# Rows scaled in place and turned by plain transposes at the start of an encoder layer

## The chip, the core and the metric

The kernel runs on one core of one Trainium2 chip. The core has five engines, each with its own queue, worked through in order: TensorE (PE, matmuls; the loading of its weights is listed apart, as PEld), VectorE (DVE), ScalarE (ACT), GpSimd (POOL) and SyncE (SP, which here only issues transfers). PE, DVE and ACT share the banks of PSUM; tiles lie in SBUF; large data lie in DRAM and come and go by DMA. The metric is the time of one execution on the device, in microseconds (us); lower is better.

## The reference

One layer of an encoder for a sequence of 1024 rows and 2048 columns, in 32-bit floats:

```
mod = silu(c) @ w_ada + b_ada;  shift, scale, gate = split(mod, 3)
h = rmsnorm(x, pre_g) * (1 + scale) + shift
proj = h @ w_in                      # q, k, v, gate_a, u, gate_p: 4608 columns
y_a = windowed_gqa(q, k, v, bias, sink) * silu(gate_a)
y_p = multiscale_pool(u) * silu(gate_p)
g = sigmoid(h @ w_merge + b_merge)   # 4096 columns
x + gate * rmsnorm((g_a * (y_a @ w_br_attn) + g_p * (y_p @ w_br_pool)) @ w_out, post_g)
```

For this case only the first two lines and the beginning of the third matter: each row of x is divided by the root of the mean of its squares, turned so that the columns lie on the partitions, and then scaled and shifted per column by numbers that are themselves sums over a 2048-row matrix.

## The kernel before, in words

**Numbers and products.** A 32-bit float is split into a high part (fp32r) and a low part, `split` (L96 on ACT, L97 on DVE), and a product is three matmuls: high by high, high by low, low by high. The large products use Strassen's scheme with seven products for a 2 by 2 block product. For that the turned rows h are kept as seven operands, `MOVING` (B11, T3, T2, B21, T4, T1, B22), each with four steps `j` of two column tiles; the weights are summed and split as they come (`strassen`, matmuls in L248). Nothing of this can start for a step `j` before its columns of x have been normed, turned and modulated (`fill`, L587, for j = 1, 2, 3; `fill_half` and `fill_sums`, L606 and L620, for j = 0).

**The start.** SP issues in this order (L655 on): the first 512 rows of x in sixteen tiles of 256 KB; sixteen tiles of w_ada for modulation group 0; four transfers of early weights (`wide`); claims of tiles; the other 512 rows of x; w_ada for group 1; raw weights for the ramp pairs 4 and 5; w_ada for group 2; raw weights 6; w_ada for group 3; raw weights 7.

A row block `si` has 128 rows and four tiles. `norm_rows` (L414) squares two of them on ACT (L419) and two on DVE (L421), adds up (L423), takes the root on ACT (L426) and the reciprocal on DVE (L427), and multiplies the identity by it (`turn`, L431). The first 512 rows are then turned by real matmuls against that scaled identity (`turn_rows`, L433, matmuls L439), which scales and transposes at once; only the first 1024 columns are turned here. A 32-bit matmul of this kind appears as two records. Of the other 512 rows, column tiles 0 and 1 are turned in the same way (`turn_first`, L449), row block by row block, and tiles 2 to 7 are scaled in place on ACT (`scale_rows`, L457) and turned later by plain transposes (`turn_later`, L463, one record each).

The sums over w_ada for a group run on PE (`modulation`, L506, matmuls named GEMV at L516), four steps of four tiles, then a copy, four transposes (PM) and three small steps on DVE; they give the columns `modc` with which h is scaled and shifted.

While data still arrive, four pairs of weight columns are multiplied with step j = 0 alone by plain blocks: `plain_block(i, nt, s)` (L691) is six matmuls (L697) into one bank, a copy to an `ev` tile on ACT (L702) or DVE (L700) in turns, and a store by SP (L703). There are eight blocks for the left half (s = 0, the first 512 rows) and eight for the right half (s = 1). Before the change the order is written out from L706 to L760: in the left half two blocks, then one row block's norm, turn and scaling, and so on; in the right half the blocks stand between transposes, the sums of step 0 (`fill_sums`) and the four steps of modulation group 1.

Then `fill(1)` makes the operands of j = 1, and the ramp runs Strassen pairs 4 to 7 with j = 0 and 1 (L768), with steps of modulation groups 2 and 3 called at numbered places (`late_sums`, L673, through `side`); then all eight pairs with the remaining steps j (L777), whose raw weights are asked for at L771; after that everything runs from full operands.

**What sets the order.** Each engine works through its queue in order. An instruction wrapped in `keep` stays in program order among those kept; all others are placed by the framework, where it expects their inputs and their tile to be ready. The norms, turns, plain blocks and their copies are kept, as are the raw weights of the ramp; stores, `fill(1)`, the weight sums and splits of the ramp pairs and the small POOL memsets with which tiles are claimed (L585) are not. Tiles are shared: the pool `big` has 56 slots of 256 KB, in which x, w_ada and the operands follow one another, so a load waits until the earlier user of its slot is done. The pool `ev` has nine tiles for results on their way out. Of PSUM, the tags `mm` and `sc` have two banks each and the two tags in `SEEDED` one each.

```
        for q in (2, 3, 0, 1):
            xt, junk = xts[si, q], xts[si, q | 2]
...
                    keep(nc.tensor.matmul(banks[j][:, m * P:(m + 1) * P], xts[4 * s + m, q][:, j * P:(j + 1) * P],
                                          turn[4 * s + m], start=True, stop=True))
...
        ps = bank(("mm", "sc")[blocks[0] % 2], "PB")
```

Of the kernel before, what the change touches and what calls it, by code (L numbers as in the profile page):

```python
# [13 lines left out]
F32 = mybir.dt.float32  # L14
F32R = mybir.dt.float32r
AF = mybir.ActivationFunctionType
ALU = mybir.AluOpType
# [4 lines left out]
P = 128  # L22
# [16 lines left out]
SEEDED = ("z0", "z1")  # L39
# [4 lines left out]
def encoder_layer(ctx: ExitStack, tc: tile.TileContext, x, c, table, w_ada, b_ada, pre_g,  # L44
# [15 lines left out]
    nc = tc.nc  # L60
# [30 lines left out]
    def keep(ins):  # L91

        tc.keep_in_program_order(ins)
# [314 lines left out]
    def fetch_rows_of_x(s):  # L408
        for si in range(4 * s, 4 * s + 4):
            for q in range(4):  # L410
                xts[si, q] = slot("xt", F32)
                load(xts[si, q], x[si * P:(si + 1) * P, q * 512:(q + 1) * 512])

    def norm_rows(si):  # L414
        ssq = ep.tile([P, 8], F32, tag="ssq", name=f"ssq{si}", bufs=4)
        for q in (2, 3, 0, 1):
            xt, junk = xts[si, q], xts[si, q | 2]
            if q % 2 == 0:
                keep(nc.scalar.activation(junk, xt, AF.Square, accum_out=ssq[:, q:q + 1]))  # L419
            else:  # L420
                keep(nc.vector.scalar_tensor_tensor(junk, xt, 1.0, xt, op0=ALU.mult, op1=ALU.mult,  # L421
                                                    accum_out=ssq[:, q:q + 1]))
# [3 lines left out]
        keep(nc.scalar.activation(ssq[:, 5:6], ssq[:, 4:5], AF.Sqrt, bias=eps_t, scale=1.0 / D))  # L426
        keep(nc.vector.reciprocal(rstd[:, si:si + 1], ssq[:, 5:6]))  # L427
# [5 lines left out]
    def turn_rows(s):  # L433

        for q in range(2):
            banks = [bank(t, "XT1") for t in ("mm", "mm", *SEEDED)]
            for m in range(4):
                for j in range(4):
                    keep(nc.tensor.matmul(banks[j][:, m * P:(m + 1) * P], xts[4 * s + m, q][:, j * P:(j + 1) * P],  # L439
                                          turn[4 * s + m], start=True, stop=True))  # L440
            for j in range(4):
                if j % 2 == 0:
                    keep(nc.vector.tensor_copy(xT[q * 4 + j, s], banks[j]))
                else:
                    keep(nc.scalar.activation(xT[q * 4 + j, s], banks[j], AF.Copy))

    late_banks = {}

    def turn_first(m):  # L449

        for k in range(2):
            if m == 0:
                late_banks[k] = bank(SEEDED[k], "XT1")
            keep(nc.tensor.matmul(late_banks[k][:, m * P:(m + 1) * P], xts[4 + m, 0][:, k * P:(k + 1) * P],
                                  turn[4 + m], start=True, stop=True))

    def scale_rows(si):  # L457

        for q, c0 in ((0, 2 * P), (1, 0)):
            part = xts[si, q][:, c0:512]  # L460
            keep(nc.scalar.activation(part, part, AF.Copy, scale=rstd[:, si:si + 1]))

    def turn_later(k, n):  # L463

        pt = bank(SEEDED[n % 2], "XT2")
        for m in range(4):
            keep(nc.tensor.transpose(pt[:, m * P:(m + 1) * P], xts[4 + m, k // 4][:, k % 4 * P:(k % 4 + 1) * P], ident))
        if n % 2:
            keep(nc.vector.tensor_copy(xT[k, 1], pt))
        else:  # L470
            keep(nc.scalar.activation(xT[k, 1], pt, AF.Copy))

    def ada_tile(j, q):
        at = xa.tile([P, 2, 4, P], F32, tag="xa", name=uid("ada"))
# [22 lines left out]
    def ada_slots(j, kcs=range(KT)):  # L497
        tiles = []
        for kc in kcs:
            tiles.append(slot("ada", F32, (P, 4, P)))  # L500
            load(tiles[-1].rearrange("p (g h) n -> p g (h n)", g=2),
                 w_ada[kc * P:(kc + 1) * P, 0:2 * D].rearrange("p (g n) -> p g n", g=2)
                 [:, :, j * 256:(j + 1) * 256])
        return tiles
# [101 lines left out]
    def fill_half(s):  # L606

        names = ("B11", "B21") if s == 0 else ("B12", "B22")
        for k, name in enumerate(names):
            src = xT[k, 0] if s == 0 else late_banks[k]  # L610
# [5 lines left out]
            keep(nc.vector.tensor_scalar(xT[k, s], src, modc[:, 1, k, 0:1], modc[:, 0, k, 0:1],  # L616
                                         op0=ALU.mult, op1=ALU.add))
            keep(sub(lo, xT[k, s], f32(hi)))
# [39 lines left out]
    fetch_wide(1)  # L658
    claim(0)
    fetch_rows_of_x(1)  # L660
# [13 lines left out]
    side = deque((lambda n=n: [step() for step in late_sums.get(n, ())]) for n in range(26))  # L674

    for si in range(4):
        norm_rows(si)
# [10 lines left out]

    blocks = [0]

    def plain_block(i, nt, s):  # L691

        ps = bank(("mm", "sc")[blocks[0] % 2], "PB")
        whi, wlo = (w[:, :, nt * P:(nt + 1) * P] for w in weights0[i])
        mov = (op["B11"][0], op["B21"][0]) if s == 0 else (right["B12"], op["B22"][0])
        for n, (kh, w, m) in enumerate(((0, whi, 0), (0, wlo, 0), (1, whi, 0), (1, wlo, 0), (0, whi, 1), (1, whi, 1))):
            keep(nc.tensor.matmul(ps, w[:, kh], mov[kh][m], start=n == 0, stop=n == 5, skip_group_check=True))  # L697
        t = ev.tile([P, 512], F32, tag="ev", name=uid("c"))
        if blocks[0] % 2:
            keep(nc.vector.tensor_copy(t, ps))  # L700
        else:
            keep(nc.scalar.activation(t, ps, AF.Copy))  # L702
        store(block(ramp_d[i], 0)(f"{nt + 1}{s + 1}"), t)  # L703
# [5 lines left out]
    wide_weights(0)  # L709
    fill_half(0)  # L710
    wide_weights(1)
    norm_rows(4)
    plain_block(0, 0, 0)
    plain_block(0, 1, 0)
    turn_first(0)
    scale_rows(4)
    wide_weights(2)
    plain_block(1, 0, 0)
    norm_rows(5)
    plain_block(1, 1, 0)  # L720
    turn_first(1)
    scale_rows(5)
    wide_weights(3)
    plain_block(2, 0, 0)
    norm_rows(6)
    plain_block(2, 1, 0)
    turn_first(2)
    scale_rows(6)
    plain_block(3, 0, 0)
    norm_rows(7)  # L730
    plain_block(3, 1, 0)
    turn_first(3)
    fill_half(1)
    scale_rows(7)
    early.close()
    late_k = deque(enumerate(range(2, 8)))

    def turn_next(n):
        for _ in range(n):
            m, k = late_k.popleft()  # L740
            turn_later(k, m)

    plain_block(0, 0, 1)
    turn_next(1)
    plain_block(0, 1, 1)
    turn_next(1)
    fill_sums(0)
    plain_block(1, 0, 1)
    turn_next(2)
    plain_block(1, 1, 1)  # L750
    turn_next(2)
    s0, s1, s2, s3, _ = modulation(1, ada[1].__getitem__, True)
    plain_block(2, 0, 1)
    s0()
    plain_block(2, 1, 1)
    s1()
    plain_block(3, 0, 1)
    s2()
    s3()
    plain_block(3, 1, 1)  # L760
# [920 lines left out]
```

## Time and profile before

| what | value |
|---|---|
| median of 3 runs | 2131.82 us (2131.21 to 2134.06) |
| the profiled execution: its time | 2135.61 us |
| its span in the trace | 2133.8 us |
| PE busy | 2079.5 us, 97% of the span |
| DVE busy | 1554.5 us, 73% |
| ACT busy | 1111.6 us, 52% |
| POOL busy | 33.3 us, 2% |
| moved by DMA | 474.49 MB, mean 222 GB/s |

The profile comes from one execution; its times count from the span's start. Rows of the chain read: start, length, engine, tile and line. Rows of the timeline read: start, length, engine, line, operation, output and inputs, count, and in brackets the idle time before and what ended it. Rows of groups read: line, engine, operation, output and inputs, shape, count, then busy microseconds and the mean nanoseconds of one, then idle time before and its releaser. Rows of the windows read: stretch, length, busy microseconds and instruction counts of PE, PEld, DVE, ACT and POOL, the clock granted to PE (1.00 is full speed), the DMA share and GB/s. Rows of transfers read: destination and source, issuing queue, count, size of one, median us from issue to landing. SPq is SP's queue.

### The profile page before, as it was taken

The numbers are of one execution on the slowest core, as the hardware profiler recorded it, in microseconds if no ns is written. First come the engines' busy times: TensorE is split into PE (matmuls) and PEld (weight loads), VectorE is DVE, ScalarE is ACT, GpSimd is POOL, SyncE is SP. The second block draws the span as 40 slices with busy tenths as digits, with TensorE's granted clock in tenths as the row PEclk, the third lists the DMA queues.
The fourth block names the chain that finished last, engine by engine and source line by source line (L and its number), as shares of the span: only waits on it lengthen the run. The fifth ranks groups of instructions, "written<-read, shape, count | busy, mean of one in ns | idle before, by whom it ended". The sixth has DMA issues, their size and how long they took to land.

```text
span 2133.8 us, 28930 instructions
## 1 busy us (share of the span) xinstructions
PE 2079.5 (97%) x9493; PEld 1709.6 (80%) x9493; DVE 1554.5 (73%) x2790; ACT 1111.6 (52%) x2111; POOL 33.3 (2%) x119
## 2 busy tenths in 40 slices
PE   6789999999999999999999999999999999999998
PEld 4558888788888888888888888888888788888886
DVE  4666778787656686577777777867957977879667
ACT  5553444444475454566665533433655645767654
POOL 0000000000000000000000000010000000000000
PEclk8999999999999999999999999999999999999999
DMA  9855877998776456445555477675754556685897
GB/s 321 270 187 196 266 261 243 321 339 294 232 237 224 132 172 208 152 160 179 176 183 161 139 222 230 220 239 182 243 168 159 183 192 198 212 319 199 299 331 246
DMA packets 305196, 474.49 MB, mean 222 GB/s; under 512 B 24324, under 2 KB 144236, under 8 KB 305045
## 3 DMA queue, kind: packets, MB, share of 16 engines
q1 hardware_dynamic: 299968, 459.89, 64.9%
q0 software_dynamic: 3616, 10.53, 1.3%
q10 hardware_dynamic: 1460, 2.22, 0.3%
q8 instruction: 74, 1.21, 0.2%
q14 instruction: 78, 0.63, 0.1%
HBM read 344.60 MB, written 130.05 MB: 222 GB/s over the span
## 4 chain that ended last, share of the span: by engine, by line
PE 92%; DMA 4%; DVE 3%; ACT 1%; issue 0%; SPq 0%; DVEq 0%; POOL 0%; ACTq 0%; POOLq 0%
PE Z L248 30%; PE X L248 20%; PE V L248 20%; PE Z L1388 2%; PE Z L1390 2%; PE Z L1389 2%; PE X L1389 1%; PE X L1390 1%; PE X L1388 1%; PE V L1389 1%; PE V L1388 1%; PE V L1390 1%; PE PT L1098 1%; DMA ada<-in_w_ada_dram 1%; PE PB L697 1%; DMA xt<-in_x_dram 1%
## 5 line engine op out<-in xcount | busy, mean ns | idle before, releaser
L96 ACT ACTIVATE whi<-raw 128x512 fp32r<-128x512 f32 (+2 forms) x528 | 319.3, 606 | 529.7 <-PE Z L248 261.3
L97 DVE TENSOR_TENSOR wlo<-raw,whi 128x512 fp32r<-128x512 f32 (+2 forms) x528 | 344.2, 655 | 172.1 <-PE Z L248 133.2
L97 DVE TENSOR_TENSOR wlo<-wr,whi 128x512 fp32r<-128x512 f32 x224 | 150.4, 688 | 53.4 <-ACT whi L96 50.7
L96 ACT ACTIVATE whi<-wr 128x512 fp32r<-128x512 f32 x224 | 138.3, 629 | 88.9 <-DVE wlo L97 29.3
L114 DVE TENSOR_TENSOR raw<-raw,raw 128x512 f32<-128x512 f32 (+1 forms) x80 | 54.6, 683 | 75.8 <-DMA raw<-in_w_merge_dram 56.7
L248 PE MATMUL X<-B11h,whi 128*128 128x512 f32 x332 | 91.6, 394 | 9.1 <-ACT whi L96 8.2
L96 ACT ACTIVATE whi<-ws 128x512 fp32r<-128x512 f32 (+2 forms) x88 | 53.4, 607 | 77.2 <-PE X L248 66.4
L114 DVE TENSOR_TENSOR u<-V,u 128x512 f32<-128x512 f32 x94 | 64.6, 687 | 38.6 <-PE V L248 37.6
L248 PE MATMUL V<-T3h,whi 128*128 128x512 f32 x332 | 91.3, 394 | 1.3 <-ACT whi L96 1.3
L248 PE MATMUL Z<-T1h,whi 128*128 128x512 f32 x332 | 90.6, 390 | 1.8 <-ACT u L258 1.8
L248 PE MATMUL Z<-T2h,wlo 128*128 128x512 f32 x332 | 89.8, 390 | 1.3 <-DVE wlo L97 1.3
L248 PE MATMUL Z<-T2h,whi 128*128 128x512 f32 x332 | 90.1, 391 | 0.9 <-ACT Z L286 0.8
L248 PE MATMUL X<-B11l,whi 128*128 128x512 f32 x332 | 90.9, 392 | 0.1
L248 PE MATMUL Z<-B22h,whi 128*128 128x512 f32 x332 | 90.5, 392 | 0.0
L248 PE MATMUL X<-B21h,whi 128*128 128x512 f32 x332 | 90.4, 391 | 0.0
L248 PE MATMUL X<-B11h,wlo 128*128 128x512 f32 x332 | 90.3, 392 | 0.0
L248 PE MATMUL V<-T4h,whi 128*128 128x512 f32 x332 | 90.2, 391 | 0.0
L248 PE MATMUL V<-T3l,whi 128*128 128x512 f32 x332 | 90.2, 390 | 0.0
L248 PE MATMUL V<-T4l,whi 128*128 128x512 f32 x332 | 89.9, 390 | 0.0
L248 PE MATMUL Z<-B22l,whi 128*128 128x512 f32 x332 | 89.8, 390 | 0.0
L248 PE MATMUL Z<-T1l,whi 128*128 128x512 f32 x332 | 89.8, 389 | 0.0
L248 PE MATMUL X<-B21l,whi 128*128 128x512 f32 x332 | 89.8, 390 | 0.0
(371 smaller groups left out, 4879.9 us busy)
## 6 DMA issues: line engine op xcount, KB each, us to landing
part<-part_d SPq DMA_DIRECT2D x136, 256.0 KB, 4.5
ada<-in_w_ada_dram SPq DMA_DIRECT2D x128, 256.0 KB, 5.8
raw<-in_w_merge_dram SPq DMA_DIRECT2D x64, 512.0 KB, 5.4
wr<-ws_dS SPq DMA_DIRECT2D x60, 512.0 KB, 5.2
raw<-in_w_in_dram SPq DMA_DIRECT2D x56, 512.0 KB, 4.0
wr<-in_w_out_dram SPq DMA_DIRECT2D x48, 512.0 KB, 5.0
proj_d<-part SPq DMA_DIRECT2D x68, 256.0 KB, 2.3
sw<-in_w_out_dram SPq DMA_DIRECT2D x64, 256.0 KB, 5.2
```

The lines of the kernel that those rows point to most:

```text
L96: ins = (nc.scalar.activation(hi, src, AF.Copy), nc.vector.tensor_tensor(lo, src, f32(hi), ALU.subtract))
L97: nc.vector.tensor_tensor(lo, src, f32(hi), ALU.subtract))
L114: return (eng or nc.vector).tensor_tensor(o, a, b, ALU.add)
L248: nc.tensor.matmul(ps, w_[:, i], op[mov][j][m_], start=fresh and i == 0 and n == 0, stop=i == nj - 1 and n == 2, skip_group_check=True)
L697: keep(nc.tensor.matmul(ps, w[:, kh], mov[kh][m], start=n == 0, stop=n == 5, skip_group_check=True))
L1098: nc.tensor.transpose(pt[:, i * P:(i + 1) * P], p[:, i * P:(i + 1) * P], ident)
L1388: nc.tensor.matmul(pb, hi, w[0], start=first, stop=False, skip_group_check=True)
L1389: nc.tensor.matmul(pb, lo, w[0], start=False, stop=False, skip_group_check=True)
L1390: nc.tensor.matmul(pb, hi, w[1], start=False, stop=last, skip_group_check=True)
```

## The change

Seven things change, all in the start of the kernel. (1) Rows are scaled in place, two tiles of a row block that are turned, one on DVE and one on ACT (`scale_rows`), and all turning is by plain transposes against the unscaled identity (`turn_part`, `take_turned`). (2) For the first 512 rows, the transposes of column tiles 0 to 3 run row block by row block, one row block behind the norms, and those of tiles 4 to 7 follow. (3) In the left half the eight plain blocks follow each other on PE with no turning between; the turning of column tiles 0 and 1 of the other rows comes behind them all. (4) In the left half a row block's squares stand ahead of the copies of the blocks; a block's copy is on ACT or DVE by `nt`. In the right half every copy and every turned tile is taken by ACT. (5) The plain blocks' results are stored by GpSimd instead of SP. (6) The first two of the four early weight transfers are issued ahead of w_ada for group 0, and the splits of the first two weight pairs stand ahead of its sums. (7) The steps of modulation groups 2 and 3 are called earlier in the ramp.

```diff
+        return ssq
+
+    def scale_rows(si, ssq):
         keep(nc.vector.reciprocal(rstd[:, si:si + 1], ssq[:, 5:6]))
-        if si % 4 == 0:
-            turn["all"] = ev.tile([P, 512], F32, tag="ev", name=uid("turn"))
-        turn[si] = turn["all"][:, (si % 4) * P:(si % 4 + 1) * P]
-        keep(nc.vector.tensor_scalar(turn[si], ident, rstd[:, si:si + 1], None, op0=ALU.mult))
...
+        keep(nc.vector.tensor_scalar(xts[si, 0], xts[si, 0], rstd[:, si:si + 1], None, op0=ALU.mult))
+        keep(nc.scalar.activation(xts[si, 1], xts[si, 1], AF.Copy, scale=rstd[:, si:si + 1]))
+
+    tbanks = {}
+
+    def turn_part(s, m, ks, tags):
+
+        for k, tag in zip(ks, tags):
             if m == 0:
...
+                tbanks[s, k] = bank(tag, "XT1")
+            keep(nc.tensor.transpose(tbanks[s, k][:, m * P:(m + 1) * P],
+                                     xts[4 * s + m, k // 4][:, k % 4 * P:(k % 4 + 1) * P], ident))
+
+    def take_turned(s, k, by_vector):
+
+        if by_vector:
+            keep(nc.vector.tensor_copy(xT[k, s], tbanks[s, k]))
         else:
...
+            keep(nc.scalar.activation(xT[k, s], tbanks[s, k], AF.Copy))
...
     fetch_rows_of_x(0)
+    fetch_wide(0)
     ada = [ada_slots(0)]
-    fetch_wide(0)
     fetch_wide(1)
...
-    late_sums = {13: group2[:1], 16: group2[1:4], 17: group2[4:], 23: group3[:4], 25: group3[4:]}
...
+    late_sums = {6: group2[:1], 8: group2[1:4], 9: group2[4:], 16: group3[:4], 18: group3[4:]}
...
+    ahead = None
+    for si in range(5):
+        done = ahead
+        ahead = norm_rows(si) if si < 4 else None
+        if done is not None:
+            scale_rows(si - 1, done)
+            turn_part(0, si - 1, range(4), ("mm", "mm", "sc", "sc"))
+    for k in range(4):
+        take_turned(0, k, k % 2)
+    for ks, tags in (((4, 5), SEEDED), ((6, 7), ("mm", "mm"))):
+        for m in range(4):
+            turn_part(0, m, ks, tags)
+        for k in ks:
+            take_turned(0, k, k % 2)
     bias_rows()
-    turn_rows(0)
...
-        store(block(ramp_d[i], 0)(f"{nt + 1}{s + 1}"), t)
         blocks[0] += 1
 
+        def put_by():
+            t = ev.tile([P, 512], F32, tag="ev", name=uid("c"))
+            if by_vector:
+                keep(nc.vector.tensor_copy(t, ps))
+            else:
+                keep(nc.scalar.activation(t, ps, AF.Copy))
+            nc.gpsimd.dma_start(block(ramp_d[i], 0)(f"{nt + 1}{s + 1}"), t)
+
+        return put_by
+
+    wide_weights(0)
+    wide_weights(1)
     g0 = modulation(0, ada[0].__getitem__, True)
...
+    for m in range(4):
+        if m < 2:
+            wide_weights(2 + m)
+        ssq = norm_rows(4 + m)
+        for nt in range(2):
+            plain_block(m, nt, 0, nt == 1)()
+        scale_rows(4 + m, ssq)
+    for m in range(4):
+        turn_part(1, m, (0, 1), SEEDED)
     fill_half(1)
...
+    def turn_next(ks):
+        for m in range(4):
+            turn_part(1, m, ks, SEEDED)
+        for k in ks:
+            take_turned(1, k, False)
+
+    plain_block(0, 0, 1)()
+    turn_next((2, 3))
+    plain_block(0, 1, 1)()
     fill_sums(0)
...
+    plain_block(1, 0, 1)()
+    plain_block(1, 1, 1)()
+    turn_next((4, 5))
     s0, s1, s2, s3, _ = modulation(1, ada[1].__getitem__, True)
...
+    plain_block(2, 0, 1)()
     s0()
...
+    plain_block(2, 1, 1)()
     s1()
...
+    plain_block(3, 0, 1)()
     s2()
...
+    last = plain_block(3, 1, 1)
+    s3(last)
+    turn_next((6, 7))
```

More of the change, by code (lines that the diff above doesn't have):

```diff
@@ L426, in norm_rows @@
         keep(nc.scalar.activation(ssq[:, 5:6], ssq[:, 4:5], AF.Sqrt, bias=eps_t, scale=1.0 / D))
+        return ssq
+    def scale_rows(si, ssq):
         keep(nc.vector.reciprocal(rstd[:, si:si + 1], ssq[:, 5:6]))
-        if si % 4 == 0:
-            turn["all"] = ev.tile([P, 512], F32, tag="ev", name=uid("turn"))
-        turn[si] = turn["all"][:, (si % 4) * P:(si % 4 + 1) * P]
-        keep(nc.vector.tensor_scalar(turn[si], ident, rstd[:, si:si + 1], None, op0=ALU.mult))
[L433 to L445, printed above, removed]
@@ L447, in encoder_layer @@
-    late_banks = {}
-    def turn_first(m):
-        for k in range(2):
-            if m == 0:
[L453 to L469, printed above, removed]
+        keep(nc.vector.tensor_scalar(xts[si, 0], xts[si, 0], rstd[:, si:si + 1], None, op0=ALU.mult))
+        keep(nc.scalar.activation(xts[si, 1], xts[si, 1], AF.Copy, scale=rstd[:, si:si + 1]))
+    tbanks = {}
@@ L672, in encoder_layer @@
     group3 = modulation(3, ada3.__getitem__, True, True)
-    late_sums = {13: group2[:1], 16: group2[1:4], 17: group2[4:], 23: group3[:4], 25: group3[4:]}
-    side = deque((lambda n=n: [step() for step in late_sums.get(n, ())]) for n in range(26))
-    for si in range(4):
-        norm_rows(si)
+    late_sums = {6: group2[:1], 8: group2[1:4], 9: group2[4:], 16: group3[:4], 18: group3[4:]}
+    side = deque((lambda n=n: [step() for step in late_sums.get(n, ())]) for n in range(19))
+    ahead = None
[12 more added lines that the diff above has]
+            take_turned(0, k, k % 2)
     bias_rows()
-    turn_rows(0)
     keep(nc.vector.tensor_scalar(nsink_t, sink_t, -1.0, None, op0=ALU.mult))
```

52 lines of the change are left out of this document (2 added, 50 removed).

## The prediction

> **What bounds the kernel now.** I read the busy time by stages first, to see where TensorE (PE) is idle at all; its columns are the stretch, then busy microseconds and instruction counts of PE, weight loads, VectorE (DVE), ScalarE (ACT), GpSimd (POOL), then granted clock, DMA share and GB/s.
>
> ```profile
> span 2133.8 us, 28930 instructions
> ...
> 0.00:147.80 147.80, 105.55 (x512) 71.34 (x512) 84.91 (x200) 79.71 (x168) 3.72 (x48) 0.93 0.80 265
> 147.80:1000.00 852.20, 850.39 (x3852) 703.94 (x3852) 602.80 (x1024) 415.30 (x788) 6.95 (x15) 1.00 0.68 226
> 1000.00:2000.00 1000.00, 997.86 (x4581) 831.06 (x4580) 774.02 (x1415) 545.92 (x1020) 16.18 (x44) 1.00 0.61 203
> ```
>
> After 147.8 us PE works 1848 of 1852 us (850.39 + 997.86): there the kernel is bound by its matmuls, none of which the change touches. Before it PE is idle 42.2 us (147.80 - 105.55). So what the edit is worth is how much earlier the point at 147.80 comes; behind it nothing gives the time back, for PE has no idle time there. Next I read the chain that ended last, in order of time (start, length, what).
>
> ```profile
> 22.15 7.14 PE XT L439 x40
> 29.29 3.69 PE GEMV L516 x32
> ...
> 35.02 0.82 ACT B11h L571
> ...
> 37.77 0.70 DVE B21l L117
> ...
> 48.07 0.71 PE XT L454 x4
> 48.78 1.39 PE PB L697 x6
> ...
> 58.97 0.79 ACT B12h L571
> ...
> 62.88 0.50 PE PB L697
> 63.38 0.44 PE XT L467 x4
> ...
> 79.42 0.99 PE GEMV L516 x8
> ...
> 141.34 5.86 DMA raw<-in_w_in_dram
> ...
> 147.80 4.21 PE X L248 x9
> ```
>
> It cuts the start into four. To 35.02: x arrives, is turned, the first modulation group is summed (GEMV). From 35.02 to 58.97: the left half, eight blocks; the chain steps from a row's turning (48.07) to a block (48.78, 1.39 for six matmuls) and back, because the next turn waits for that row's norm, which stands behind a copy of a block. From 58.97 to 88.54: the right half, where turning goes on between the blocks. Then the four Strassen pairs, and the wait for raw weights that ends at 147.80. The right half ends where the second block of rows of the operands is filled. The timeline has it with what ended an engine's idle time in brackets, and before it the transposes that stood 5.38 us for ACT's copies, which were queued behind the sums:
>
> ```profile
> 75.62 1.97 PE L467 MATMUL XT<-ident,xt 128*128 128x128 f32 x8 [5.38 <-ACT xT L471]
> ...
> 88.54 1.52 ACT L571 ACTIVATE xT<-xT,modc 128x512 f32<-128x512 f32 x2 [1.35 <-DVE modc L494]
> ```
>
> **Turning the first half.** Today 20 of the 32 scaled matmuls run after the last norm, 7.14 us. Plain transposes cost 0.11 each (63.38: four in 0.44), three quarters of the first sixteen run while later rows arrive, so PE is free for the GEMV about 4 us sooner, near 25 (the last row's scaling ends near 22.6, twenty transposes take 2.2, one copy frees a bank). That gains nothing by itself, for the data of the GEMV are late:
>
> ```profile
> 12.77 12.94 SPq L501 DMA_DIRECT2D ada<-in_w_ada_dram  x16
> ...
> ada<-in_w_ada_dram SPq DMA_DIRECT2D x32, 256.0 KB, 6.0
> ```
>
> Sixteen tiles leave SyncE (SP) 0.81 apart, the last at 24.9, and land 6.0 later, 30.9. The change puts two early weight transfers of the same size ahead of them: 32.5. The last quarter of the GEMV (3.69/4 = 0.9) can then end at 33.5; now it ends at 32.98. Cost 0.5 us. What the early weights buy, their splits before the GEMV, was beside ACT's first modulation anyway: nothing. The scaling in place lies under the wait for the next rows of x, except for the last row, whose share is in the 22.6.
>
> **The left half, 23.95 us now (58.97 - 35.02).** Groups of instructions between 35 and 89 us (busy, mean ns of one | idle before):
>
> ```profile
> L421 DVE SCALAR_TENSOR_TENSOR xt<-xt 128x512 f32<-128x512 f32 x8 | 5.5, 687 | 0.1
> L700 DVE COPY c<-PB 128x512 f32<-128x512 f32 x7 | 4.8, 685 | 4.0 <-PE PB L697 4.0
> L702 ACT ACTIVATE c<-PB 128x512 f32<-128x512 f32 x8 | 4.7, 594 | 10.2 <-PE PB L697 10.2
> L97 DVE TENSOR_TENSOR wlo<-wide,whi 128x256 fp32r<-128x256 f32 x8 | 3.0, 420 | 0.9 <-ACT whi L96 0.9
> L616 DVE TENSOR_SCALAR xT<-xT,modc 128x512 f32<-128x512 f32 x2 | 1.1, 542 | 0.3 <-ACT B11h L571 0.3
> L427 DVE RECIPROCAL rstd<-ssq 128x1 f32<-128x1 f32 x4 | 0.7, 164 | 1.4 <-ACT ssq L426 1.4
> ```
>
> With all eight blocks next to each other on PE, and squares ahead of copies, DVE sets the end. From the start of B11h it needs 3.45 until B21l is out (37.77 + 0.70), four weight splits (4 x 0.42 = 1.7), and per row two squares, one copy, a reciprocal and the scaling: 2 x 0.687 + 0.685 + 0.164 + 0.542 = 2.77, plus an estimated 0.4 for the reduction, the reads of the sums and the hand-overs, so 3.17, four times: 12.7. I add 0.8 for the second block, which is late for its first copy while PE's clock is at half (an estimate; the clock's row stands below), and 0.4 for the last transposes. Sum 19.0: gain 4.9. ACT (two squares, one copy, one scaling per row) has less. PE needs eight blocks, 11.1 at full clock; four banks let it run four blocks ahead of the copies. The rows of x are there: the last is the twentieth transfer after the 30.9, at 0.81 each 47.1, and its squares are due near 51. Net of the 0.5, B12h starts 4.4 us earlier.
>
> **The right half, 29.57 us now.** The order is written out, so PE's list can be summed. First block as now, 4.4 (58.97 to 63.38). Seven blocks at 1.39: 9.7. Sixteen transposes at 0.11: 1.8. Four GEMV steps at 0.99: 4.0. From the end of the GEMV to the fill as in the first half, 2.0 (32.98 to 35.02). Sum 21.9. The last eight transposes run under that tail. The 5.38 us that PE now stands before 75.62 go, because the transposes of parts 2 and 3 are copied out before the sums, and those of 4 and 5 find empty banks; ACT, which takes over all copies of this half, has eight at 0.59, six turned tiles at 0.6, four splits and two modulations, under 14 of 22 us. What can be late next is PE's clock.
>
> ```profile
> 37.70:44.50 6.80, 6.18 (x17) 4.63 (x17) 5.54 (x16) 3.19 (x9) 0.00 (x0) 0.51 1.01 356
> 51.30:54.70 3.40, 1.67 (x9) 1.31 (x9) 2.08 (x7) 2.24 (x7) 0.20 (x2) 1.00 1.10 348
> ```
>
> In the first stretch PE was busy 6.18 of 6.80 us and still had half the clock, after a stretch with little to do. In the new order PE idles some 2 to 3 us before 54.6, while DVE ends the last row, so the clock may fall as the right half begins. Bounds: nothing, as in the second stretch, half busy and at full clock, and 3.4 us, half of such a stretch. I take 1.0, since the first block waits for DVE anyway. That makes 22.9, gain 6.7. [...]
>
> **Stores by GpSimd.** Sixteen stores leave SP's queue.
>
> ```profile
> 55.80 21.15 SPq L703 DMA_DIRECT2D ramp_d<-c  x12
> 77.04 10.59 SPq L501 DMA_DIRECT2D ada<-in_w_ada_dram  x16
> ...
> 103.03 6.26 DMA ramp_d<-c
> ...
> L248 PE MATMUL Z<-T1h,whi 128*128 128x512 f32 x6 | 2.0, 408 | 1.4 <-ACT u L258 1.4
> ```
>
> Twelve of them hold SP from 55.80 to 76.95, but the loads behind them need slots that the second GEMV frees, so they gain nothing by the free queue alone: they move with the GEMV. The last four stand behind loads, and until one lands (103.03 + 6.26) a Strassen pair has no tile: PE waits 1.4. Strassen stores remain on SP, so between 0 and 1.4 I take 0.7. GpSimd's own price:
>
> ```profile
> out_dram<-mo POOLq DMA_DIRECT2D x8, 256.0 KB, 6.3
> ...
> out_dram<-mo SPq DMA_DIRECT2D x8, 256.0 KB, 2.4
> ...
> L1422 POOL DMA_DIRECT2D out_dram<-mo x8 | 4.3, 539 | 39.4 <-DVE mo L1421 39.4
> ```
>
> 0.54 to issue, 6.3 to landing against 2.4: sixteen in some 34 us use 9 us of a queue that also carries 14 small memsets. Nobody waits for a landing unless all nine output tiles are out. Summation groups 2 and 3 are called 7 or 8 steps earlier; their loads start some 9 us earlier as well, so I count them at nothing. The gap before 147.80 keeps its cause: raw weights leave SP behind the last pair's last store.
>
> **Sum.** 4.4 + 6.7 + 0.7 = 11.8. The profiled execution has a span of 2133.8 and took 2135.6; 2122.0 and 2123.8 would follow. The median of the runs, 2131.8, is 3.8 below that execution: 2120.0.
>
> **Rivals.** *The raw weights of the second pass move up.* The page's group of the first matmuls of a pair has their largest wait:
>
> ```profile
> L248 PE MATMUL X<-B11h,whi 128*128 128x512 f32 x332 | 91.6, 394 | 9.1 <-ACT whi L96 8.2
> ```
>
> Only pinned instructions keep their order; the framework places the rest. If these loads leave before the last stores, up to the 8.2 us that PE stands before 147.80 for these splits go too: 2111.8. For it: SP has free stretches, and the tiles are free by then. Against: the edit does not touch that code.
>
> *DVE meets the Strassen weights too early.* The sums of pair 4's weights are not pinned and stand in DVE's queue right behind the right half's B22l:
>
> ```profile
> 62.75 0.42 DVE L117 TENSOR_TENSOR ws<-raw 128x256 f32<-128x256 f32 x1
> ...
> 52.74 2.63 SPq L198 DMA_DIRECT2D raw<-in_w_in_dram  x4
> ...
> raw<-in_w_in_dram SPq DMA_DIRECT2D x4, 256.0 KB, 5.8
> ```
>
> Those weights land about 61 now (52.74 + 2.63 + 5.8). In the new order DVE is there at 58.5 (54.6 + 62.88 - 58.97), while eight GpSimd stores of 256 KB at 348 GB/s, 0.75 each, go first: 67. DVE would stand 8.5 us. The splits and copies behind it have about 4 us of slack on PE's list, so some 5 reach PE: 2125; without slack 2128.5.
>
> *GpSimd's queue becomes the bound.* Store k is out at 42 + kh, landed 5 later, h being the queue's time per store. The 25th output tile is wanted about 96 and needs the 16th store landed: it decides from h = 3.1, and eats the whole gain at 3.8. With 4.5, some eight times the row, the tile is 23 late: 2143. For it: one queue in order, with memsets that wait for tiles of x. Against: DVE worked 774 of 1000 us in the stretch from 1000 us on, and stores there took 0.54. [...]
>
> **Chances.** Forecast 0.63, on its own 2116 to 2124 (clock term 0 to 3.4, stall 0 to 1.4, a few DVE hand-overs). Raw weights earlier 0.10. DVE meeting weights early 0.20, a third of it above 2127.5. GpSimd's queue 0.05. The rest, 0.02, is a planner's order that cancels the gain. 0.2% is 4.3 us, about what a measurement of this kernel can tell from no change. Faster by more: 0.63 + 0.10 + 0.13 = 0.86; within: 0.09; slower: 0.05. The range 2112 to 2127 takes in the whole first rival and most of the second.
>
> **What would show it.** Right: the first GEMV ends near 33.5 although PE is free near 25; B12h starts near 54.6; the right half's blocks follow without a gap over 1 us; the fill of operand block 1 starts near 77.4; matmuls of pair 4 near 79.5; PE idle before the steady stage near 30 instead of 42.2. Wrong in a step: DVE idle before a weight sum with the raw DMA as releaser; a granted clock of 0.5 past 62; GpSimd stores over 1 us each or copies waiting for a store; PE waiting at a GEMV for its tiles. Wrong as a whole: the steady stage not starting 9 us or more earlier.

## The result and the profile after

The changed kernel takes 2126.13 us in the median of 7 runs (2123.70 to 2127.22), the kernel before 2131.82 (7 runs, 2131.10 to 2135.03). The medians differ by 5.7 us. The ratio, which takes in all runs (their means are 2125.56 and 2132.54), is 0.9967, 95% interval 0.9956 to 0.9979: 7.0 us less, between 4.5 and 9.4. The profiled execution of after has a span of 2124.5 us (2126.26 with what lies around it), 9.3 less than that of before.

First the busy time by stages; columns as in the prediction.

```profile
0.00:138.79 138.79, 105.78 (x471) 68.66 (x471) 83.10 (x195) 83.14 (x175) 11.95 (x64) 0.91 0.83 281
138.79:1000.00 861.21, 858.38 (x3894) 711.12 (x3895) 609.43 (x1042) 420.81 (x800) 6.96 (x15) 1.00 0.68 225
```

The steady stage starts at 138.79 instead of 147.80, 9.0 earlier, and from there to the end it takes 1985.7 us against 1986.0. So the whole difference lies ahead of that point: PE idles there 33.0 us (138.79 - 105.78) instead of 42.2. The granted clock of that stretch is lower than before (0.91 against 0.93), and that is where some of the gain went. The chain that ended last, in order of time (start, length, what):

```profile
25.16 7.58 PE GEMV L494 x32
...
34.79 0.82 ACT B11h L549
...
52.99 0.50 DVE xt L431
...
53.90 0.79 ACT B12h L549
...
57.82 0.80 PE PB L686
58.61 1.71 PE XT L441 x8
...
78.23 0.82 ACT xT L549
...
79.43 0.59 ACT xT L449
80.02 0.70 ACT xT L549
...
84.03 1.19 PE V L248 x2
85.23 1.28 PE Z L248 x3
...
130.65 0.61 ACT u L303
...
131.28 0.70 DVE p L114
...
132.00 0.32 SPq L326
...
132.37 5.83 DMA raw<-in_w_in_dram
...
138.22 0.53 ACT whi L96
...
138.79 4.21 PE X L248 x9
```

Cut at the same four places as before:

| stretch | before | after | gained | forecast |
|---|---|---|---|---|
| to the start of B11h | 35.02 | 34.79 | 0.23 | -0.5 |
| left half, to B12h | 23.95 | 19.11 | 4.84 | 4.9 |
| right half, to the fill of block 1 | 29.57 | 24.33 | 5.24 | 6.7 |
| fill to steady stage | 59.26 | 60.56 | -1.30 | 0.7 |

Two rows are short of the forecast, and in both PE has half its clock. Four stretches of the changed kernel's trace, cut near the places where the granted clock changes (it is the column behind POOL's; the cuts lie 0.24 behind the changes, hence 0.97 and 0.52 in place of 1.00 and 0.50):

```profile
51.55:54.96 3.41, 1.20 (x8) 0.73 (x7) 1.84 (x7) 3.00 (x7) 1.07 (x2) 0.97 1.07 399
54.96:61.79 6.83, 6.25 (x19) 4.64 (x20) 4.65 (x7) 2.07 (x4) 1.01 (x12) 0.52 1.08 380
78.86:82.27 3.41, 1.91 (x5) 0.86 (x6) 2.60 (x5) 3.41 (x8) 0.00 (x0) 0.96 1.09 389
82.27:89.10 6.83, 6.52 (x15) 4.63 (x16) 5.33 (x10) 4.32 (x11) 0.00 (x0) 0.52 1.10 353
```

A stretch of 3.41 us in which PE had little to do (1.21 and 1.72 us of work, when cut at the change itself) is followed by 6.83 us at half clock although PE is then busy for nearly all of it: at most 3.4 us lost each time. In the chain it is seen as pairs that cost 1.28 per three matmuls at 85.23, where 0.69 is usual. The half clock ends at a boundary of 3.41 us behind a stretch filled with work (3.41 us of it in the steps from 58.14 and from 85.44). The chain also has ACT's copies of two turned tiles (ACT xT L449) between the two modulations of the filled block.

The gap ahead of the steady stage is as long as before, and its cause is now bare. In the last lines of the chain the last Strassen pair's result is copied (130.65) and summed (131.28), its store leaves SP (132.00), and only behind it do the raw weights of the second pass leave (132.37); they land at 138.20, ACT splits them, PE goes on. PE's wait there is 8.2 us in both kernels (8.18 and 8.21).

### The profile page after: what moved, and what is told of

It reads as the page before. It is cut to its first block, busy times and chain, and to the rows that moved or that the text cites. A ratio compares the mean times of both kernels' runs of the same rounds, so it can differ in the third digit from the quotient of the medians.

```text
span 2124.5 us, 28858 instructions
## 1 busy us (share of the span) xinstructions
PE 2079.3 (98%) x9453; PEld 1706.7 (80%) x9453; DVE 1551.5 (73%) x2783; ACT 1114.9 (52%) x2118; POOL 41.7 (2%) x135
## 3 DMA queue, kind: packets, MB, share of 16 engines
q8 instruction: 74, 1.21, 0.2%
## 4 chain that ended last, share of the span: by engine, by line
PE 92%; DVE 3%; DMA 3%; ACT 1%; issue 1%; SPq 0%; DVEq 0%; ACTq 0%
PE Z L248 30%; PE V L248 20%; PE X L248 20%; PE Z L1367 2%; PE Z L1369 2%; PE Z L1368 2%; PE V L1369 1%; PE X L1368 1%; PE X L1369 1%; PE V L1368 1%; PE V L1367 1%; PE X L1367 1%; PE GEMV L494 1%; PE PT L1077 1%; PE PB L686 1%; DMA xt<-in_x_dram 1%
## 5 line engine op out<-in xcount | busy, mean ns | idle before, releaser
L248 PE MATMUL Z<-T2l,whi 128*128 128x512 f32 x332 | 90.2, 391 | 0.0
L248 PE MATMUL V<-T3h,wlo 128*128 128x512 f32 x332 | 90.1, 391 | 0.0
```

The costliest lines, as they stand in the source:

```text
L248: nc.tensor.matmul(ps, w_[:, i], op[mov][j][m_], start=fresh and i == 0 and n == 0, stop=i == nj - 1 and n == 2, skip_group_check=True)
```

## The experiments

Theory A, from the traces: the gain is the left half (squares ahead of copies, blocks next to each other) and the right half without its stall; the stores, the early weights and the earlier summations hardly count; what is missing went to PE's clock; the gap ahead of the steady stage is SP's order and nothing else. The rivals are that the stores by GpSimd make the change, that the summations' earlier places do, or that the gap has another cause. Eleven kernels were run, in three sets, each set beside the kernel before on its chip (2135.51, 2134.59 and 2132.63 us); ratios are to that kernel, intervals are 95%. "After" has 0.9967.

### The stores back on SP

```
-            nc.gpsimd.dma_start(block(ramp_d[i], 0)(f"{nt + 1}{s + 1}"), t)
+            store(block(ramp_d[i], 0)(f"{nt + 1}{s + 1}"), t)
```

> The changed kernel with the sixteen stores of the plain blocks on SyncE's queue again, nothing else undone. Theory A (the order of the left half and the written-out right half bring the gain, the stores little): the left half's B12h still starts near 53.9 us and the fill of operand block 1 near 78.2; a Strassen pair waits for a tile again, 1 to 2 us; the steady stage starts 0 to 2 us later than 138.8, the time is 0 to 2 us above the changed kernel. Rival B (freeing SyncE's queue is the gain): the fill or the pairs slip by 4 us or more and the time goes back to about 2131.

Measured: 2143.23 us (2142.55 to 2143.93), ratio 1.0038 (1.0023 to 1.0053): slower than the kernel before. To B12h at 53.58 nothing differs; then SP's queue has this (timeline of this run: start, time, queue, line, what, count):

```profile
54.44 3.33 SPq L695 DMA_DIRECT2D ramp_d<-c  x5
...
69.45 0.46 SPq L695 DMA_DIRECT2D ramp_d<-c  x1
70.95 8.62 SPq L479 DMA_DIRECT2D ada<-in_w_ada_dram  x14
...
89.42 4.13 SPq L479 DMA_DIRECT2D ada<-in_w_ada_dram  x6
93.90 1.11 SPq L198 DMA_DIRECT2D raw<-in_w_in_dram  x2
95.40 6.71 SPq L695 DMA_DIRECT2D ramp_d<-c  x10
```

Ten of the sixteen stores stand behind loads, which wait for their slots; stores are not kept in program order, and the framework put them there. All nine output tiles are then out, and ACT and PE stand (timelines of both engines, idle time and releaser in brackets):

```profile
101.14 0.60 ACT L694 ACTIVATE c<-PB 128x512 f32<-128x512 f32 x1 [14.53 <-DMA ramp_d<-c]
```

```profile
102.28 1.29 PE L742 MATMUL OPEN<-B11h 128*128 128x512 f32 x2 [15.27 <-ACT xT L449]
```

The steady stage starts at 155.27, 16.5 later than after. On this point theory A falls: the stores are no small term, in this order of blocks and loads they make the difference between a gain and a loss. The time that SP spends on issuing them is not enough for that: sixteen issues of 0.32 (as for the store at 132.00 in the chain of after) are 5.1 us; the 16.5 are the time for which a queue that works in order holds finished stores behind loads that cannot start yet.

### The kernel before with the stores by GpSimd

```
-        store(block(ramp_d[i], 0)(f"{nt + 1}{s + 1}"), t)
+        nc.gpsimd.dma_start(block(ramp_d[i], 0)(f"{nt + 1}{s + 1}"), t)
```

> The kernel before, with one part of the change alone: its sixteen stores of plain blocks are issued by GpSimd instead of SP; order, squares, transposes and early loads are those of before. Theory A (the stores are an enabler: in the old order copies are spread over 60 us, so SP's queue cost them little): the start to 88.5 us stays as before within 1 us, the 1.4 us that PE stood in a Strassen pair for a tile whose store landed at 109.3 go, the steady stage begins 1 to 2 us earlier than the 147.80 of before, ratio 0.999 to 1.000. Theory B (the stores are the change: the twelve that held SP from 55.80 to 76.95 held the loads behind them): the loads of the second group of modulation and the raw weights land some 5 us or more earlier, the steady stage begins near 140, ratio 0.996 to 0.997.

Measured: 2131.52 us, ratio 0.9988 (0.9979 to 0.9998), some 2.6 us. The wait of 1.40 for a store's landing near 110 is gone, the steady stage starts at 145.16, 2.6 earlier. Of that 0.8 is an earlier B11h (34.23), which is within that row's scatter, 1.1 a shorter left and right half, and 0.7 lies behind the fill. The fill (86.64) is 1.9 earlier, where theory A allowed 1, but the result is much nearer to A than to B: alone, in the old order, the stores are worth some 2 us. Together with the run above: they pay because the rest of the change needs them.

### The summations back at their old places in the list

```
-    late_sums = {6: group2[:1], 8: group2[1:4], 9: group2[4:], 16: group3[:4], 18: group3[4:]}
+    late_sums = {13: group2[:1], 16: group2[1:4], 17: group2[4:], 23: group3[:4], 25: group3[4:]}
```

> The changed kernel with the steps of modulation groups 2 and 3 called at the old places (13, 16, 17, 23, 25). Theory A: no change before the ramp; the steady stage starts within 1 us of 138.8, because what ends last before it is the raw weights behind the last store, not the operands; the last fill runs about 10 us later on VectorE and ScalarE and ends beside the wait for the raw weights. Rival D (the earlier sums matter by themselves): the steady stage starts 3 us or more later.

Measured: 2126.32 us, ratio 0.9960 (0.9945 to 0.9975), the same as after. The raw weights leave at 132.06, the steady stage starts at 137.63, 1.2 before that of after; the half clock at 82 to 89 did not come in this execution. Nothing starts later for the old places: the earlier ones are worth nothing while that gap stands, as forecast.

### The squares behind the copies again

```
     for m in range(4):
...
-        ssq = norm_rows(4 + m)
         for nt in range(2):
             plain_block(m, nt, 0, nt == 1)()
+        ssq = norm_rows(4 + m)
```

> The changed kernel with one order undone: in the left half a row block's squares stand behind the copies of its two plain blocks, on both engines; the blocks stay together on TensorE. Theory A (VectorE's queue sets the left half, and the first copies wait for blocks at half clock): the left half grows from 19.1 to 21 to 23 us, B12h starts 2 to 4 us later, and the steady stage follows by the same. Rival E (that the blocks follow each other on TensorE is the whole of it): the left half stays within 0.5 us of 19.1.

Measured: 2128.74 us, ratio 0.9972 (0.9961 to 0.9983). In the medians this is not told apart from after; in the trace the left half takes 22.45 us (35.98 to 58.43) instead of 19.11. So 3.3 of the 4.84 of that stretch are the order of squares and copies; the other 1.5 belong to the rest of the new left half (plain transposes, blocks next to each other, copies by `nt`), which no run takes apart. The steady stage starts at 141.24, 2.4 later, but 1.2 of that is a later B11h: not all of the 3.3 reaches it.

### Work of no use where PE would idle

Six matmuls, of which nothing is read, ahead of the last row's turning, eight behind the right half's last block.

```
+        if m == 3:
+            warm(6, op["B11"][0][0])
...
+    warm(8, op["B11"][0][0])
```

> The changed kernel with matmuls added whose results nobody reads: six before the last two transposes of the left half, eight behind the two opening matmuls that follow the right half. Theory A (TensorE's clock falls to half after each of these two idle places, from 55.0 to 61.8 and from 82.3 to 89.1 us, and that costs the right half about 1.4 and the ramp about 2.5 us): full clock in both, fill of operand block 1 near 77, steady stage 2 to 4 us earlier than 138.8, time 2 to 4 us below the changed kernel. Rival C (VectorE and ScalarE set the pace there and the clock costs nothing): steady stage within 1 us of 138.8 or, by the added work, up to 2 us later.

Measured: 2125.16 us, ratio 0.9953 (0.9936 to 0.9969), not told apart from after. The steady stage starts at 137.37, 1.4 earlier, less than the 2 to 4 of theory A. Three stretches of this run, cut as above:

```profile
51.66:55.07 3.41, 2.82 (x16) 1.89 (x14) 2.37 (x8) 2.97 (x8) 1.49 (x4) 1.00 1.07 386
55.07:58.48 3.41, 1.91 (x5) 0.78 (x5) 2.71 (x4) 1.19 (x2) 0.31 (x1) 0.97 1.08 403
58.48:61.90 3.42, 3.16 (x12) 2.85 (x13) 2.19 (x4) 1.44 (x3) 1.01 (x12) 0.54 1.05 383
```

The added work fills the stretch to 55.07, and the clock holds; the next one, in which PE waits for the splits of B12 and B22, has 1.91 of work, and the clock falls one step later, for half as long. The half clock at 82 to 89 did not come. Nor did it in five runs of the new order without added matmuls (it came in after and two others), so the added work can't be credited with that. What decides it is seen in the next run but one.

### The early weights behind the first summation's tiles

```
-    fetch_wide(0)
     ada = [ada_slots(0)]
+    fetch_wide(0)
     fetch_wide(1)
```

> The changed kernel without one part: the first half of the early weights is loaded behind the sixteen tiles of the first summation again, as before. The prediction: the first summation ends 0.5 sooner (its tiles land two transfers of 256 KB earlier), the left half begins near 34.2 to 34.5, and the splits of the early weights, which then stand behind the modulation, cost nothing. Rival: the splits of the early weights now stand on ACT and DVE ahead of the left half's first blocks, and with the weights later they fall between the modulation and the blocks, so the left half is 1 to 2 us longer than 19.1. Either is under 0.1% of the time; the trace decides, not the median.

Measured: 2124.82 us, ratio 0.9960 (0.9946 to 0.9974), no difference from after. Neither expectation had the place right (timelines of ACT, then of PE):

```profile
30.97 0.42 ACT L96 ACTIVATE whi<-wide 128x256 fp32r<-128x256 f32 x1 [5.38 <-DMA wide<-in_w_in_dram]
31.65 1.03 ACT L96 ACTIVATE whi<-wide 128x256 fp32r<-128x256 f32 x3 [0.27 <-DMA wide<-in_w_in_dram]
32.59 0.57 ACT L501 ACTIVATE acc<-GEMV 128x512 f32<-128x512 f32 x1
```

```profile
33.22 0.66 PE L462 MATMUL PM<-ident,acc 128*128 128x128 f32 x4 [1.86 <-ACT acc L501]
```

The summation ends at 31.36 (33.22 - 1.86), 1.4 sooner than after; but the weights' splits stand ahead of the copy of its result in ACT's queue, wait for late data and hold it for 1.2. B11h starts at 34.92, as with the early weights. The left half takes 18.37, not more. So in this one execution the early load costs on SP what it saves on ACT.

### The raw weights of the second pass by GpSimd

```
-    def ramp_raws(i, js):
-        raws.append(load_raws(*weight_of(RAMP_ORDER[i]), rows_in_turn(0), js, True))
+    def ramp_raws(i, js, load=load):
+        raws.append(load_raws(*weight_of(RAMP_ORDER[i]), rows_in_turn(0), js, True, load))
...
-        ramp_raws(i, (1, 2, 3) if i in A else (2, 3))
+        ramp_raws(i, (1, 2, 3) if i in A else (2, 3), nc.gpsimd.dma_start if i < 2 else load)
```

> The changed kernel, with the raw weights of the first two pairs of the second pass issued by GpSimd instead of SP, where they stand behind the last pair's last store. Theory A (that place in SP's queue alone makes the gap ahead of the steady stage, as the prediction's last paragraph on stores had it and as the last wait of ACT and DVE at 138.2 for the raw DMA has it): the raw weights land before 125, PE's wait of 8.2 us ahead of the steady stage goes but for about 1, the steady stage begins 130 to 132 instead of 138.79, and without that idle time the half clock at 133.5 to 143.7 does not come either, which is worth up to 4 us more behind it; time 2114 to 2119. Rival (their slots are free only late, or the splits of operand blocks and ACT's own queue are as late): GpSimd waits for the slots, the steady stage begins within 2 us of 138.8, time within 2 us of the changed kernel's. Second rival (they land early but take the DMA share of the group-2 and group-3 sums): steady stage about 135, time about 2122.

Measured: 2114.92 us (2113.79 to 2115.45), ratio 0.9907 (0.9892 to 0.9922): 0.6% under after. GpSimd's timeline, then the chain:

```profile
92.41 0.78 POOL L198 DMA_DIRECT2D raw<-in_w_in_dram  x1 [12.73 <-DVE wlo L97]
106.56 0.76 POOL L198 DMA_DIRECT2D raw<-in_w_in_dram  x1 [13.37 <-DMA ramp_d<-c]
120.97 0.75 POOL L198 DMA_DIRECT2D raw<-in_w_in_dram  x1 [13.65 <-DVE wlo L97]
```

```profile
125.80 1.36 PE X L248 x6
...
129.88 2.04 PE X L248 x9
```

The slots come free at 92, 107 and 121; in SP's queue these loads left from 132.37 on. PE goes from the last pair into the steady stage without a gap, and at full clock: nine matmuls in 2.04 where after took 4.21. From the next group of this kind on it is 11.4 ahead of after (137.36 against 148.75). Theory A, whole.

This run shows the clock at the right half's end too. The added matmuls are not in it, PE's work from the right half's last block to the first pairs is that of after, and yet:

```profile
78.07:81.48 3.41, 2.16 (x14) 1.48 (x13) 2.24 (x7) 2.54 (x6) 0.54 (x1) 1.00 1.08 391
81.48:84.89 3.41, 2.27 (x7) 0.97 (x6) 2.64 (x5) 3.41 (x8) 0.00 (x0) 1.00 1.08 377
84.89:88.31 3.42, 2.79 (x12) 2.29 (x13) 3.42 (x7) 2.89 (x7) 0.00 (x0) 1.00 1.10 350
```

Here the idle time lies across two stretches of the grid, each keeps over 2 us of work, and the clock stays; in after it fell into one.

### The same on the kernel before

> The kernel before, with one edit alone that is no part of the change: the raw weights of the first two pairs of the second pass are issued by GpSimd instead of SP. On the changed kernel the same edit took 11.2 us off the median and moved the start of the steady stage from 138.79 to 129.88. Theory A (that gap was there in both kernels and is independent of the change): the steady stage begins some 8 to 10 us before 147.80, ratio 0.9955 to 0.996, so the change and this edit add up. Theory B (the gap can be taken away only because the change moved the summations of groups 2 and 3 ahead: in the kernel before the last modulation of operand blocks ends at about 149, behind the raw weights, so that it holds the steady stage next): the steady stage begins at 144 or later, ratio 0.998 to 1.000.

The edit is the one above. Measured: 2126.96 us, ratio 0.9970 (0.9957 to 0.9983). PE's timeline:

```profile
138.12 0.61 PE L248 MATMUL Z<-T1h,wlo 128*128 128x512 f32 x2
138.57 0.62 PE L248 MATMUL X<-B11h,whi 128*128 128x512 f32 x2
```

The second pass starts at 138.57, 9.2 earlier, with no gap, and its span is 2122.9, 10.9 less than before. In the traces the two edits add up: the second such group starts at 158.27 before, 148.75 with the change (9.5), 146.75 with this edit (11.5), 137.36 with both (20.9). So the gap is no part of the change (theory A); the ratio, though, lies between the two expectations. By the ratios this edit gives 6.4 us here and some 13 on top of the change (0.9907 by 0.9967). The two traces flatter it here: the profiled execution of before lies 3.0 above the median of the kernel before on this chip, and the one of this kernel is the fastest of its five, with a mean granted clock of 0.997 against 0.994 to 0.995 in the other four. What those four lost, no trace shows; that the gains add up holds for the traces alone.

### Turned tiles 6 and 7 copied by DVE

```
-    turn_next((6, 7))
+    turn_next((6, 7), True)
```

> The changed kernel, with the last two turned tiles of the right half (6 and 7) copied out by DVE instead of ACT. In the changed kernel ACT's two copies stand between the two modulations of the filled block, 79.0 to 80.0. Theory A (that costs the 1.05 us by which the first split after the fill starts late, and the pairs behind it are late by it): the first split of the operand block starts 0.5 to 1 us sooner after the fill, but the gap ahead of the steady stage, which is a wait for raw weights behind the last store, passes the 0.5 to 1 on; ratio 0.9960 to 0.9967. Rival (DVE is then the later of the two engines, its modulation waits behind the copies): the same or up to 1 us later, ratio 0.997.

Measured: 2124.55 us, ratio 0.9959 (0.9945 to 0.9973). Inconclusive: the steady stage starts at 135.80, but in that execution the clock did not fall at 82, which is more than the copies can be worth.

### Combinations

> The changed kernel with both additions: fourteen matmuls of no use on PE where it would idle (six before the last two transposes of the left half, eight behind the right half's last block), and the raw weights of the second pass's first two pairs issued by GpSimd. If the gap ahead of the steady stage goes with the raw weights (theory A of the run with that alone) and the half clock at 82 to 89 goes with the added matmuls, the steady stage begins at 128 to 131, and the time is 2112 to 2118, the least of all kernels here. If only the raw weights count, it is within 1.5 us of the run with those alone. If the half clock falls where it will, whatever stands there, the two differ by chance alone, up to 3 us either way.

> The changed kernel with two additions: the second pass's first raw weights by GpSimd, and the turned tiles 6 and 7 copied by DVE instead of ACT. With the raw weights alone the fill of the operand block began at 79.71 and the first split at 82.25, behind ACT's two copies. If those two copies were on the path, the first split comes 1 us sooner after the fill, and as the gap behind is gone the steady stage begins 0.5 to 1 us sooner as well: time 2113.5 to 2114.5. If PE's own list holds the pairs (it has no idle time from 85 on), the same: 2114 to 2116.

Measured: added matmuls and raw weights by GpSimd 2115.11 us, ratio 0.9910 (0.9895 to 0.9924); DVE's copies and raw weights by GpSimd 2113.79 us, ratio 0.9909 (0.9896 to 0.9923). Neither is told apart from the raw weights alone; the ratios of all three are 0.0057 to 0.0060 under that of after, some 12 us. In the second the steady stage starts 94.0 behind B11h (129.79 - 35.75) instead of 94.7, as if the two copies were worth 0.7; but in the first, which has not these copies, it starts 94.1 behind (128.91 - 34.77). What the copies are worth is not shown.

## Why the prediction held, and where its sum was too large

**The cause was right.** The time is gained ahead of the steady stage and nowhere else, by the left and right half, and nothing behind gives it back. The order of squares and copies and the stores were each put back alone. The right half's old order was not: that its stall is gone is read from the trace, in which PE waits nowhere between B12h and the fill longer than 0.76 us, where before it stood 5.38.

**The first summation, 0.5 cost.** B11h starts at 34.79, not 35.5. One execution can't tell: over the nine profiled kernels with the early weights it starts between 34.64 and 35.98, 35.24 in the mean; over the three that have before's start (before and its two variants) at 34.23 to 35.02, 34.72 in the mean. The difference is 0.5, under a scatter of 1.3. The step "what the early weights buy: nothing" failed in its reason: they keep ACT free for 1.2 us, which the run with the later weights shows.

**The left half, 19.0.** It took 19.11, DVE's list as summed, and the run with the squares behind the copies took 22.45.

**The right half, 22.9.** It took 24.33, and two terms were too small. PE's list, summed to 21.9, lacks 0.8: a GEMV step with the block behind it takes 2.58 (steps start at 69.91 and 72.49), where the sum has 0.99 and 1.39, and it took as long before the change (79.35 and 81.94). The other 1.6 lie ahead of 62.17 and are the term for the clock. It was bounded by 0 and 3.4 and taken as 1.0 "since the first block waits for DVE anyway". In the nine other kernels with the new order the right half takes 23.9 to 25.7, with 3.4 to 13.7 us at half clock in it or just ahead; less the list with its 0.8 that is 1.2 to 3.0. So 1.0 was too small each time, because the idle time of PE ahead of the right half is part of the new order and comes each time. The stretch ahead of this fall held 1.21 us of PE's work (51.31 to 54.72 in after), and in the traces every step at full clock with up to 1.54 was followed by half clock (the counts stand in the last section). In the kernel before, the clock once came back behind work that was mostly transposes: from 75.02 to 78.44 PE, at half clock, was busy for 2.82 us, 1.97 of them eight transposes, and the next step had the full clock; in no trace did the full clock, between 20 and 160 us, come back behind less work than that.

**Stores, 0.7, and what follows the fill.** As a term of its own it was of the right size (1.4 of PE's wait went). As a step it failed: it stood in the sum as a small extra, while the other 11.1 hang on it. The working saw that the stores "move with the GEMV", and did not ask what SP would hold if blocks came faster than the loads ahead of them. From the fill to the steady stage the forecast had the 0.7; after lost 1.30. In the four kernels that keep the gap and in which the half clock at 82 to 89 did not come (old places, squares behind copies, added matmuls, DVE's copies) the stretch takes 57.4 to 58.6 instead of 59.26, a gain of 0.7 to 1.9; with it, in after, 60.56, which is 2.0 to 3.2 more (with it for one step alone, in the run with the later weights, 58.2). The prediction had no term for it, though it named a granted clock of 0.5 past 62 as a sign against itself.

**GpSimd, the weights' sums, the second pass.** Stores by GpSimd took 0.54 each, the first 0.58, while DVE was busy 14.90 of 20 us (34 to 54), as in the row that the prediction went by; the rival of GpSimd's queue did not come. DVE did not stand for raw weights in the right half: behind B22l it went on with sums of the operand. The raw weights of the second pass did not move up, as held against the first rival, and when made to they gave more than its 8.2 us, since the clock no longer falls there either.

**The sum.** 11.8 was forecast, 9.3 came in the traces: 1.4 lost in the right half and 2.0 behind the fill, 0.7 and 0.3 better at the start and in the steady stage. The rest of the distance, 2120.0 against 2126.13, is the step that takes the median "3.8 below that execution": the profiled execution of after lies at its median (2126.26 against 2126.13), that of before 3.8 above its own. It rested on one execution, which was slower than all seven of the kernel before beside after.

**What was luck.** The forecast's own range was 2116 to 2124, and 2126.13 lies outside it. It lies in 2112 to 2127 only through the room left for the second rival, which did not come. The sign for the whole, a steady stage 9 us earlier, was met by 9.0, and an execution can shift that point by more than 1 us, as B11h's scatter shows.

## What to carry to other kernels

An engine's queue that works in order has to be read as a list whenever an edit makes its producers faster: finished stores behind loads that wait for slots turned 9 us of gain into 8 us of loss, and a critical load behind a store that comes late cost 11 in the changed kernel, which no edit of the arithmetic could reach. Ask of each gap ahead of a busy stage which issue stood ahead of the load that ended it, and whether another queue is free. Where an order makes PE wait for some 2 us out of 3.4, give the half clock that follows a term in the sum: of at most 3.4 us it cost 1.6 in one place here and 2.0 to 3.2 in the other.

## What the runs showed of the chip

In the traces the clock is granted on a grid: all changes between 20 and 154 us lie a whole number of 3.41 us apart in each trace (in after, 54.72 to 61.55 is two steps, 133.23 to 143.47 three), and the phase differs from execution to execution. In after, 1.72 us of work in 3.41 was no protection (the stretch ahead of 82.03).

The thirteen traces, cut at their own grids between 20 and 160 us, show how much work holds the clock. Of their steps at full clock, all 26 with up to 1.54 us of PE's work were followed by half clock; with 1.55 to 1.97 it was 13 of 21; with 2.03 or more, none of 375. Of the steps at half clock, none with less than 2.8 us of work was followed by full clock, and all with 3.1 or more were. So the same idle time makes the clock fall or not by how it lies on the grid (in after, one step with 1.72 of work, and it fell; in the run with the raw weights by GpSimd, two steps with 2.16 and 2.27, and it stayed). This scatter is of the order of the effects that the medians here could not tell apart.
